# When the second and third piece of one split operand are prepared: with the first or with the second Strassen product of a down projection

## The chip, the cores and the metric

The kernel runs on one core of one Trainium2 chip, as a single launch. The metric is the device time of that launch in microseconds (us); lower is better. Times of whole runs and one profiled execution are used. All instants below are microseconds from the start of the profiled span.

## The reference

One layer of a hybrid encoder on 512 positions of width 1024: a normalised input projection, three token mixers with gates, an output projection with a residual, and then a SwiGLU feed-forward block. The change lies in the last product, `act @ w_ffn_down`, with `D_FF` = 2816:

```python
h2 = rms_norm(x, norm_ffn[l])
act = jax.nn.silu(jnp.einsum('bsd,df->bsf', h2, w_ffn_gate[l])) * jnp.einsum('bsd,df->bsf', h2, w_ffn_up[l])
x = x + jnp.einsum('bsf,fd->bsd', act, w_ffn_down[l])
```

Everything is float32.

## The kernel before

**Products in two parts.** A float32 operand is split into a high part `h`, rounded to the matmul's format by ScalarE (ACT), and a low part `l` = operand − `h`, taken by VectorE (DVE). A product is then three matmuls: high by high, high by low, low by high. Weights are split by `split_a` (lines 1379 and 1380), which writes the pairs named `whd…` and `wld…`; activations of the down projection are split by `split_d2` (lines 1400 and 1401), which writes the tiles named `Bd…`.

**Seven products instead of eight.** The first 256 rows of `w_ffn_down` are multiplied plainly (`fd`, results in `ps_d`). The other 2560 rows are done with a Strassen–Winograd scheme on two by two blocks: products in the order `DORDER` = 11, 12, S1, S2, S3, S4, 22. A product uses five sets of weights (n = 0 to 4) and one split activation operand in three pieces (kh = 0, 1, 2, which hold 4, 4 and 2 slices of 128 rows). Each product is done for two halves of the output, q = 0 and q = 1. In each half three uses of sets stand (`USE`): q = 0 takes sets 0, 1 and the first half of 2, q = 1 the second half of 2, then 3 and 4. A whole set is 24 matmuls of 128x256, a half set 12. `ps_dy` and `ps_dx` are their sums in PSUM.

**Where the activation operands come from.** The operands of the S products are sums and differences of blocks of the activations. They are made in place (`in_place`, line 1570, five DVE instructions for each combination) and then split (`both`, three calls of `split_d2`, one for each kh). The dictionary `LATER` lists, for each product, the pieces of such work that are called while that product is emitted: after each of the three uses, two pieces for q = 0 and one for q = 1. So 9 pieces at most are called with one product; they are taken from the front of its list.

**Where the weights come from.** For products 12 and 22 the sets are loaded by plain DMAs on SyncE's queue (SP) into tiles `dr` of the pool that has three buffers under the tag `raw` (`dfetch`, line 1549). `make_d(n0 + use[0] + 3)` runs ahead of each use: it splits the sets up to three after the one in use and asks for the loads of two more. A `dr` buffer is reloaded when both halves of the split that reads it are done. The weights of the other products stand in tiles `dw`; they are turned into the next combination by DMAs that add in memory, issued by GpSimd (POOL, `dadd`, line 1537). The split weights themselves have three buffers for the high and three for the low parts.

**What sets the order.** A scheduler orders each engine's instructions from the emitted order, their dependencies and priorities. `split_d2` holds the DVE half of a split (line 1401) at its place in the emitted order for all products but 11 and 12 (`tc.keep_in_program_order`, the name `pin`); the ACT half (line 1400) is left free. `in_place` is held too. The DVE halves of the weight splits are held relative to nothing.

`x<-x,ps_dy` (line 1624) is DVE's addition of a finished block to the residual.

Of the kernel before, what the change touches and what calls it, by code (L numbers as in the profile page):

```python
# [12 lines left out]
ALU = mybir.AluOpType  # L13
# [53 lines left out]
def layer_kernel(ctx: ExitStack, tc: tile.TileContext, x, xt, vecs, w_in, w_qkv7, w_gate7, w_pool, w_rg, w_ig,  # L67
# [1184 lines left out]
    with ExitStack() as ffn:  # L1252
# [134 lines left out]
        def ablk(i, kh, j):  # L1387
            return [acts[1 + 5 * i + 2 * kh + n][:, :, j * H:(j + 1) * H] for n in range(2 - kh // 2)]

        def split_d2(nm, kh, i, j):  # L1390

            pin = tc.keep_in_program_order if nm not in ("11", "12") else lambda i: None
            if kh < 2:
                h, l = g4([4, H], f"Bd{nm}{kh}h", F32R), g4([4, H], f"Bd{nm}{kh}l", F32R)
            else:
                t = g4([2, 2, H], f"Bd{nm}{kh}", F32R)
                h, l = t[:, 0], t[:, 1]
            for n, src in enumerate(ablk(i, kh, j)):
                ns = slice(2 * n, 2 * n + 2)
                act(h[:, ns, :], src, AF.Copy)  # L1400
                pin(dve.tensor_tensor(l[:, ns, :], src, h[:, ns, :].bitcast(F32), ALU.subtract))
            DB[nm, kh] = h, l
# [165 lines left out]
        def in_place(dst, sign, op, other):  # L1568
            return [lambda kh=kh: [tc.keep_in_program_order(
                dve.scalar_tensor_tensor(t, t, sign, o, ALU.mult, op)) for t, o in zip(ablk(dst[0], kh, dst[1]), ablk(other[0], kh, other[1]))]  # L1570
                    for kh in range(3)]

        def both(nm, i, j):
            return [lambda kh=kh: split_d2(nm, kh, i, j) for kh in range(3)]
# [4 lines left out]
                   lambda: [dload("21", n, DX) for n in range(5)],  # L1579
                   lambda: [dadd("22", n, DX) for n in range(5)]] + both("12", 1, 0)[:1])  # L1580

        LATER = {"11": both("12", 1, 0)[1:] + in_place((0, 0), 1.0, ALU.subtract, (0, 1)) + both("S1", 0, 0),
                 "12": in_place((0, 0), -1.0, ALU.subtract, (1, 1)) + both("S2", 0, 0),
                 "S1": in_place((0, 1), -1.0, ALU.add, (1, 1)) + both("S3", 0, 1),
                 "S2": both("S4", 1, 1) + in_place((0, 0), -1.0, ALU.subtract, (1, 0)),
                 "S3": both("22", 0, 0)}
# [50 lines left out]
        for nm in DORDER:  # L1637
            z, half, first, adds = plan[nm]
            todo = LATER.get(nm, [])
            n0 = dsets.index((nm, 0))  # L1640
# [76 lines left out]
```

## Time and profile before

| | us |
|---|---|
| median of 3 runs | 901.95 |
| lowest and highest of them | 900.20 and 902.67 |
| the profiled execution's own time | 900.52 |
| its span, first to last instruction | 898.7 |
| PE (TensorE matmul) busy | 891.1 |
| DVE busy | 736.7 |
| ACT busy | 532.9 |
| POOL busy | 106.7 |

In a timeline a row is: start, duration, engine, line, operation, output <- inputs, shapes, count; in brackets stands how long the engine was idle before it and what released it. Rows of equal neighbours are merged ("x4"). Engines start the next instruction a little before the profile's end of the last one, so a row's distance to the next start is what it occupies. PE's busy share counts matmuls whose ends are modelled, so a matmul's row is longer than its distance to the next.

### The profile page before, as it was taken

Reading aid. Unit: us, or ns where it says so; the run is one execution under the profiler, and the core shown is the slowest. Engines: PE = TensorE matmul, PEld = TensorE weight load, DVE = VectorE, ACT = ScalarE, POOL = GpSimd, SP = SyncE. Lnnn points to the kernel's source line nnn. Section 1 sums busy time; section 2 is a strip of 40 time slices with the busy share of each in tenths; the row PEclk is TensorE's granted clock in tenths of the full one; section 3 lists DMA queues with packets and bytes.
Section 4 is the critical chain, followed back from the end, with each engine's and each line's share of the span. In section 5 each row is a group of like instructions: output and inputs, shape, how many; then the busy total and the mean of one; then the engine's idle time right before and its main releaser. Section 6 shows DMA issues by size and latency. Waiting matters only on the chain.

```text
span 898.7 us, 14578 instructions
## 1 busy us (share of the span) xinstructions
PE 891.1 (99%) x5731; PEld 802.4 (89%) x5731; DVE 736.7 (82%) x937; ACT 532.9 (59%) x747; POOL 106.7 (12%) x150
## 2 busy tenths in 40 slices
PE   9999999999999999999999999999999999998998
PEld 6888778888899888888888988999999999998998
DVE  7897897988786599967887685798888888998974
ACT  7554989556856556555664545655555555654642
POOL 1010002232332101000001100000010100121200
PEclk9999999999999999999999999999999999999999
DMA  9485347798582786634635864836666676887913
GB/s 342 141 309 150 114 132 210 220 299 244 179 262 71 234 234 192 218 118 145 214 93 154 190 179 164 258 81 174 169 148 176 162 169 201 211 210 205 196 39 117
DMA packets 83620, 164.59 MB, mean 183 GB/s; under 512 B 7904, under 2 KB 48864, under 8 KB 83552
## 3 DMA queue, kind: packets, MB, share of 16 engines
q1 hardware_dynamic: 68000, 107.29, 35.9%
q0 software_dynamic: 15408, 56.11, 28.2%
q8 instruction: 45, 0.74, 0.3%
q10 hardware_dynamic: 144, 0.26, 0.1%
q14 instruction: 23, 0.19, 0.1%
HBM read 143.19 MB, written 18.87 MB: 180 GB/s over the span
## 4 chain that ended last, share of the span: by engine, by line
PE 93%; DVE 3%; ACT 2%; DMA 1%; issue 1%; DVEq 0%; ACTq 0%; SPq 0%
PE ps_y L283 13%; PE ps_x L283 10%; PE ps_q L794 7%; PE ps_dy L1633 5%; PE ps_dx L1633 4%; PE ps_br L274 3%; PE ps_br L275 3%; PE ps_br L276 3%; PE ps_bY L1234 2%; PE ps_gy L283 2%; PE ps_gate L697 2%; PE ps_gate L276 2%; PE ps_bX L1234 2%; PE ps_gx L283 2%; PE ps_gate L274 2%; PE ps_gate L275 2%
## 5 line engine op out<-in xcount | busy, mean ns | idle before, releaser
L110 ACT ACTIVATE whi<-raw 128x1024 fp32r<-128x1024 f32 x61 | 64.6, 1059 | 73.3 <-PE ps_br L275 14.7
L111 DVE TENSOR_TENSOR wlo<-raw,whi 128x1024 fp32r<-128x1024 f32 x61 | 74.4, 1220 | 28.9 <-ACT whi L110 28.9
L111 DVE TENSOR_TENSOR wlo<-qw,whi 128x1024 fp32r<-128x1024 f32 x48 | 58.6, 1222 | 20.8 <-ACT whi L110 20.4
L110 ACT ACTIVATE whi<-qw 128x1024 fp32r<-128x1024 f32 x48 | 50.7, 1057 | 33.1 <-PE ps_q L794 18.7
L1379 ACT ACTIVATE wh<-w 128x1024 fp32r<-128x1024 f32 x34 | 36.2, 1064 | 49.4 <-PE ps_x L283 24.7
L1380 DVE TENSOR_TENSOR wl<-w,wh 128x1024 fp32r<-128x1024 f32 x34 | 41.6, 1223 | 7.3 <-ACT wh L1379 6.7
L1380 DVE TENSOR_TENSOR wl_S<-w,wh_S 128x1024 fp32r<-128x1024 f32 x30 | 36.6, 1220 | 12.1 <-ACT wh_S L1379 12.0
L1379 ACT ACTIVATE wh_S<-w 128x1024 fp32r<-128x1024 f32 x30 | 31.8, 1060 | 22.5 <-PE ps_y L283 19.8
L1379 ACT ACTIVATE whdS<-dw 128x1024 fp32r<-128x1024 f32 x20 | 21.3, 1064 | 22.1 <-PE ps_dy L1633 11.1
L1380 DVE TENSOR_TENSOR wldS<-dw,whdS 128x1024 fp32r<-128x1024 f32 x20 | 24.2, 1220 | 6.4 <-ACT whdS L1379 6.3
L1050 DVE TENSOR_TENSOR_SCAN E<-K,ahead 128x512 f32<-128x512 f32 (+3 forms) x32 | 25.3, 812 | 4.4 <-ACT K L1046 4.4
L274 PE MATMUL ps_br<-yHH,whi 128*128 128x512 f32 x64 | 25.3, 395 | 0.0
L274 PE MATMUL ps_lru<-HH,whi 128*128 128x512 f32 x64 | 25.2, 394 | 0.0
L274 PE MATMUL ps_br<-yph,whi 128*128 128x512 f32 x64 | 25.2, 394 | 0.0
L274 PE MATMUL ps_pool<-HH,whi 128*128 128x512 f32 x64 | 25.2, 393 | 0.0
L274 PE MATMUL ps_gate<-HH,whi 128*128 128x512 f32 x64 | 25.0, 391 | 0.0
L276 PE MATMUL ps_gate<-HH,wlo 128*128 128x512 f32 x64 | 25.0, 391 | 0.0
L275 PE MATMUL ps_br<-ypl,whi 128*128 128x512 f32 x64 | 25.0, 391 | 0.0
L276 PE MATMUL ps_br<-yph,wlo 128*128 128x512 f32 x64 | 25.0, 391 | 0.0
L275 PE MATMUL ps_br<-yHL,whi 128*128 128x512 f32 x64 | 25.0, 390 | 0.0
L276 PE MATMUL ps_br<-yHH,wlo 128*128 128x512 f32 x64 | 25.0, 390 | 0.0
L275 PE MATMUL ps_pool<-HL,whi 128*128 128x512 f32 x64 | 25.0, 390 | 0.0
(768 smaller groups left out, 3540.0 us busy)
## 6 DMA issues: line engine op xcount, KB each, us to landing
w<-in_w_gu_dram SPq DMA_DIRECT2D x44, 512.0 KB, 6.6
raw<-in_w_in_dram SPq DMA_DIRECT2D x31, 512.0 KB, 5.2
qw<-in_w_qkv_dram SPq DMA_DIRECT2D x24, 512.0 KB, 6.5
w<-in_w_gu_dram POOLq DMA_DIRECT2D x20, 512.0 KB, 7.3
dw<-in_w_down_dram POOLq DMA_DIRECT2D x20, 512.0 KB, 8.0
raw<-in_w_branch_dram SPq DMA_DIRECT2D x16, 512.0 KB, 4.2
qw<-in_w_qkv_dram POOLq DMA_DIRECT2D x12, 512.0 KB, 7.8
qd<-r POOLq DMA_DIRECT2D x12, 512.0 KB, 7.8
```

What stands on the lines that cost most here:

```text
L110: act(hi, raw, AF.Copy)
L111: dve.tensor_tensor(lo, raw, hi.bitcast(F32), ALU.subtract)
L274: nc.tensor.matmul(ps, lh, rh, start=start, stop=False, skip_group_check=skip)
L275: nc.tensor.matmul(ps, lh, rl, start=False, stop=False, skip_group_check=skip)
L276: nc.tensor.matmul(ps, ll, rh, start=False, stop=stop, skip_group_check=skip)
L283: nc.tensor.matmul(o, a_[a][:, w, k, :], b_[b][:, k, :], start=first and n == k == 0, stop=last and n == 2 and k == 3, skip_group_check=True)
L794: nc.tensor.matmul(ps[:, a, :], b_[:, k, ts_], a_[:, kk, :], start=first and n == k == 0, stop=n == 2 and k == 3, skip_group_check=True)
L1050: dve.tensor_tensor_scan(E[:, c0:c0 + n][:, ::-1], K[:, c0 + 1:c0 + n + 1][:, ::-1], ahead[:, S - n:][:, ::-1], 0.0, ALU.mult, ALU.add)
L1234: nc.tensor.matmul(o, ah[x_][:, w, k, :], b[k][y_], start=first_ and n == k == 0, stop=n == 2 and k == 3, skip_group_check=True)
L1379: act(h, src, AF.Copy)
L1380: dve.tensor_tensor(l, src, h.bitcast(F32), ALU.subtract)
L1633: nc.tensor.matmul(o, a_[a][:, w, k0 + k, :], b_[b][:, k, :], start=first and i == k == 0, stop=last and i == 2 and k == nk - 1, skip_grou ...
```

## The change

In `LATER`, two of the three calls that split the operand of S1 (kh = 1 and kh = 2) move from the end of the list of product 11 to the front of the list of product 12. The first (kh = 0) stays with 11. No instruction is added or removed.

```diff
-        LATER = {"11": both("12", 1, 0)[1:] + in_place((0, 0), 1.0, ALU.subtract, (0, 1)) + both("S1", 0, 0),
-                 "12": in_place((0, 0), -1.0, ALU.subtract, (1, 1)) + both("S2", 0, 0),
+        LATER = {"11": both("12", 1, 0)[1:] + in_place((0, 0), 1.0, ALU.subtract, (0, 1)) + both("S1", 0, 0)[:1],
+                 "12": both("S1", 0, 0)[1:] + in_place((0, 0), -1.0, ALU.subtract, (1, 1)) + both("S2", 0, 0),
```

The list of 11 goes from 8 pieces to 6, that of 12 from 6 to 8. As built, the queues differ only in this stretch:

- DVE, before: BdS11l (two instructions), wld120, BdS12, wld121, the addition `x<-x,ps_dy` of q = 1, wld122, four of the five in-place differences for S2, wld123, the fifth, BdS20l (two), wld124, BdS21l (two), BdS22, wldS10, wldS11.
- DVE, after: wld120, wld121, the addition, wld122, BdS11l (two), BdS12, wld123, four in-place differences, wld124, the fifth, BdS20l (two), BdS21l (two), wldS10, BdS22, wldS11.
- ACT, before: BdS10h (two), whd120, BdS11h (two), whd121, BdS12, whd122, whd123, BdS20h (two), whd124, BdS21h (two), whdS10, BdS22, whdS11.
- ACT, after: BdS10h (two), whd120, BdS11h, whd121, BdS11h, whd122, BdS12, whd123, whd124, BdS20h (two), whdS10, BdS21h (two), BdS22, whdS11.
- PE: before, two matmuls of q = 1 with set 122 stood ahead of the third matmul of product 12's first set; after, they stand with the others of set 122.
- POOL and SP: the same instructions in the same order.

(Names are product and set or piece: `wld123` is the low part of set 3 of product 12, `BdS11` piece kh = 1 of the operand of S1.)

## The prediction

> **What bounds the kernel now.** I read the page first, for the span and the chain of work that ended last; then that chain in order of time, to see where it leaves PE; then the timelines of PE, DVE and ACT there; and last the stretches with PE's clock and the DMA queues.
>
> ```profile
> span 898.7 us, 14578 instructions
> ...
> PE 93%; DVE 3%; ACT 2%; DMA 1%; issue 1%; DVEq 0%; ACTq 0%; SPq 0%
> ```
>
> The profiled execution took 900.52 us, 1.8 more than this span, and the chain is PE for 93% of it. An edit to DVE's order is worth something only where the chain leaves PE. From 780 us on that is one place, between the first two products of the down projection. PE's own rows there:
>
> ```profile
> 808.83 0.28 PE L1633 MATMUL ps_dx<-Bd120l,whd 128*128 128x256 f32 x1
> 809.96 0.51 PE L1633 MATMUL ps_dx<-Bd,whd 128*128 128x256 f32 x2 [0.85 <-ACT whd L1379]
> ...
> 817.90 0.28 PE L1633 MATMUL ps_dx<-Bd,wld 128*128 128x256 f32 x1
> 818.98 0.39 PE L1633 MATMUL ps_dx<-Bd120h,whd 128*128 128x256 f32 x1 [0.81 <-ACT whd L1379]
> 819.21 0.28 PE L1633 MATMUL ps_dx<-Bd120l,whd 128*128 128x256 f32 x1
> 820.24 0.39 PE L1633 MATMUL ps_dx<-Bd120h,wld 128*128 128x256 f32 x1 [0.76 <-DVE wld L1380]
> ...
> 827.41 0.28 PE L1633 MATMUL ps_dx<-BdS10h,wldS 128*128 128x256 f32 x1
> ```
>
> The same stretch by PE's clock:
>
> ```profile
> 817.52:820.93 3.41, 1.84 (x13) 1.44 (x13) 1.97 (x3) 2.77 (x4) 0.00 (x0) 1.00 0.61 243
> 820.93:824.37 3.44, 3.44 (x19) 3.44 (x18) 3.44 (x6) 2.89 (x5) 0.00 (x0) 0.51 0.60 166
> 824.37:828.00 3.63, 3.63 (x34) 3.63 (x34) 2.84 (x3) 1.80 (x2) 1.34 (x2) 0.99 0.33 132
> ```
>
> (Columns: stretch, length, PE, PEld, DVE, ACT, POOL busy with counts, granted clock, DMA share, GB/s.)
>
> At full clock matmuls of this size start 0.11 us apart (34 in 3.63). So PE stands three times: about 1.0 us before 809.96, 0.97 before 818.98 and 0.9 before 820.24. The last row is the third matmul of S1, the first that needs wldS10; I use it as the finish line, because from there PE runs without a stop.
>
> What PE waits for at 818.98 and 820.24 is set 123, and that set's load starts the wait:
>
> ```profile
> 810.04 7.72 DMA dr<-in_w_down_dram
> ```
>
> It is issued at 810.04 and lands at 817.76. It could not be issued earlier: its buffer is that of set 120, and was free only when DVE had made wld120. DVE's rows (I read them for what stands ahead of what):
>
> ```profile
> 806.96 0.68 DVE L1624 TENSOR_TENSOR x<-x,ps_dy 128x512 f32<-128x512 f32 x1
> 807.56 1.28 DVE L1401 TENSOR_TENSOR BdS11l<-act,BdS11h 128x512 fp32r<-128x512 f32 x2
> 808.76 1.22 DVE L1380 TENSOR_TENSOR wld<-dr,whd 128x1024 fp32r<-128x1024 f32 x1
> 809.90 0.68 DVE L1401 TENSOR_TENSOR BdS<-act,BdS 128x512 fp32r<-128x512 f32 x1
> 810.50 1.21 DVE L1380 TENSOR_TENSOR wld<-dr,whd 128x1024 fp32r<-128x1024 f32 x1
> 811.64 0.68 DVE L1624 TENSOR_TENSOR x<-x,ps_dy 128x512 f32<-128x512 f32 x1
> 812.24 1.22 DVE L1380 TENSOR_TENSOR wld<-dr,whd 128x1024 fp32r<-128x1024 f32 x1
> 813.37 2.49 DVE L1570 SCALAR_TENSOR_TENSOR act<-act,act 128x512 f32<-128x512 f32 x4
> 818.96 1.23 DVE L1380 TENSOR_TENSOR wld<-dr,whd 128x1024 fp32r<-128x1024 f32 x1 [3.10 <-ACT whd L1379]
> 820.10 0.68 DVE L1570 SCALAR_TENSOR_TENSOR act<-act,act 128x512 f32<-128x512 f32 x1
> 820.71 1.28 DVE L1401 TENSOR_TENSOR BdS20l<-act,BdS20h 128x512 fp32r<-128x512 f32 x2
> 821.91 1.22 DVE L1380 TENSOR_TENSOR wld<-dr,whd 128x1024 fp32r<-128x1024 f32 x1
> 823.05 1.28 DVE L1401 TENSOR_TENSOR BdS21l<-act,BdS21h 128x512 fp32r<-128x512 f32 x2
> 824.25 0.68 DVE L1401 TENSOR_TENSOR BdS<-act,BdS 128x512 fp32r<-128x512 f32 x1
> 824.85 2.35 DVE L1380 TENSOR_TENSOR wldS<-dw,whdS 128x1024 fp32r<-128x1024 f32 x2
> ```
>
> DVE is full here but for 3.10 us ahead of 818.96, and the four in-place differences at 813.37 are done before that gap. By the distances of starts, a weight split occupies 1.14, a half split or a difference 0.60, two of them 1.20, four 2.40.
>
> **The change, part by part.** *Wld120 moves ahead of BdS11l.* It starts at 807.56 instead of 808.76 and ends at 808.78. The load of set 123 follows 0.06 behind as now: issued at 808.84, 1.20 earlier. wld121 then stands at 808.70, and wld122 behind the addition at about 810.44. PE needs wld121 24 matmuls (2.7 us) after 808.9 and wld122 as long again after that, so both are early.
>
> *PE's stop at 809.96 goes.* It was for whd122, out of turn: two matmuls of set 122 stood ahead of the third of set 120. In the changed queue they stand in their place, and wld120 is there at 808.78. PE goes on at 808.95 and comes to set 123 1.01 earlier, at 817.00 instead of 818.01. That alone buys nothing: it lengthens the wait for set 123.
>
> *Set 123 comes earlier.* If the load takes 7.72 again, it lands at 816.56. From landing to PE's matmul with wld123 the chain is ACT, then DVE, 2.48 now (817.76 to 820.24) and 2.48 then: 819.04. Here PE is 1.20 ahead.
>
> *The differences for S2 now stand behind wld123.* This is the new wait. BdS11l and BdS12 take the place ahead of the gap (wld122 starts at 810.44, so they end by about 813.4), and DVE then waits for whd123 until 817.76 with four differences queued behind it. They are not waiting for the load, but the queue is in order. DVE's gap grows from 3.10 to over 4 us, and 2.40 of work moves behind it. Behind wld123 (at 817.76) come, in the changed order: four differences at 818.90, wld124 at 821.30, the fifth at 822.44, BdS20l at 823.04, BdS21l at 824.24, wldS10 at 825.44, done at 826.66. BdS22 (0.60) goes behind wldS10, which is already counted. PE meets this twice: at wld124 (wanted at 821.8, there at 822.52), then at wldS10 (wanted at 825.3, there at 826.66). S1's third matmul starts 0.04 later, at **826.70 instead of 827.41: 0.71 less**.
>
> ACT's halves do not bind: its rows show it waiting for data.
>
> ```profile
> 817.87 1.06 ACT L1379 ACTIVATE whd<-dr 128x1024 fp32r<-128x1024 f32 x1 [7.97 <-DMA dr<-in_w_down_dram]
> 818.84 1.14 ACT L1400 ACTIVATE BdS20h<-act 128x512 fp32r<-128x512 f32 x2
> 820.26 1.06 ACT L1379 ACTIVATE whd<-dr 128x1024 fp32r<-128x1024 f32 x1 [0.29 <-DMA dr<-in_w_down_dram]
> ```
>
> Even if set 124 landed no earlier than the 820.2 it now has, whd124 would end at 821.32, and wld124 stands at 821.30 anyway. The moved pieces themselves cost nothing later: BdS11 and BdS12 are wanted at S1's second and third set, after 829, and are made by 813.4. POOL's and SP's instructions keep their order. PE's, ACT's and DVE's work is the same, so the sum is this 0.71 and nothing else.
>
> *The clock.* The three stretches above change what 0.71 is compared with. After the two stops the clock is halved for 3.44 us, and 19 matmuls start where 34 do next. [...] Without the halving, PE in the kernel before would have used wld124 at 823.17 and wldS10 when it was done (824.85 + 1.22 = 826.07): finish line 826.11, that is 1.30 earlier. In the changed kernel a halving between 819 and 826 hides in the 2 us that PE waits for DVE anyway. So against an execution before without it, the change costs 826.70 − 826.11 = 0.59; against the profiled one it gains 0.71. A halving later, inside S1, is hidden by nothing.
>
> The unknown is the load. Around its issue the queues hold:
>
> ```profile
> 800.67 3.57 POOL L1537 DMA_DIRECT2D dw<-in_w_down_dram  x4 [12.86 <-DMA dw<-in_w_down_dram]
> ```
> ```profile
> q0 software_dynamic: 68, 0.21, 108.9%
> ```
> ```profile
> q0 software_dynamic: 57, 0.17, 86.3%
> q1 hardware_dynamic: 14, 0.06, 15.1%
> ```
> ```profile
> DMA to landing us min/median/max: 3.3/5.7/8.7
> ```
>
> The second fence is the stretch 810 to 811, the third 813 to 814: POOL's additions (q0) hold the DMA engines alone for 3 us after the issue, and only then do the load's packets (q1) begin. The last is all `dr` loads. So the load could land where it does now, 817.76, if it has to wait for the same additions; or earlier by more than 1.20, if an earlier place in the queue is worth one 512 KB addition, 0.524 MB at the 0.21 MB per us of the second fence, 2.5 us. I take its own 7.72 again.
>
> **The rivals.** *The load does not move (slower).* It waits for the additions and lands at 817.76. For it: the 3 us without a packet. Against: loads elsewhere do not wait so, down to 3.3 us. DVE's wld123 stays at 818.96 and everything behind it comes 1.20 later than in my sum: wldS10 done at 827.86, finish 827.90, 0.49 more than the profiled run, 1.79 more than one without the halving. It decides from a landing at 817.27, where my 0.71 is used up.
>
> *The halving falls into S1 (slower).* The two stops ahead of 826.70 are about 0.7 and 1.4 us, in 5 us; if one stretch of 3.4 holds as much of them as 817.52:820.93 did, S1 runs 3.44 us at half: 16 matmuls instead of 30, 1.6 us. Then +0.9 against the profiled run. Against it: the stops are further apart than now.
>
> *The load gains a whole addition (faster).* It lands 2.5 earlier, at 815.26; DVE's chain then moves 1.30 further, unless set 124 holds it: finish 825.4, 2.0 less. [...]
>
> *It does nothing.* ACT's halves hardly move, and if PE's gain ends in a stall of equal size, the time is that of before.
>
> **How the numbers follow.** Forecast 0.52; load unmoved 0.18; halving in S1 0.15; whole addition 0.10; nothing 0.05. On the profiled time: 900.52 − 0.71 = 899.81. The median of the three runs is 1.43 above that execution; the same 0.71 less than 901.95 gives **901.2**. The rivals by the same median: 902.4, 902.9, 899.9 and 902.0. Three runs of the kernel before spread over 2.47 us (0.27%), so 0.3%, 2.7 us, is about what can be told from no change. No case alone reaches it: the largest are −2.0 and, against runs of before without the halving, +1.8 (load unmoved) and +2.2 (halving in S1). Beyond it lie only these joined with the runs' own spread, or an unmoved load and a halving in S1 together (+2.1 on the profiled run). I give faster by over 0.3% 0.10, within 0.76, slower 0.14, and the range **899.0 to 904.4**: from 899.9 down by 0.9 and from 902.9 up by 1.5, for the spread.
>
> **What would show it.** In the changed profile: PE without a stop near 809; the load of set 123 issued near 808.8 and its landing; DVE idle over 4 us ahead of wld123 with four L1570 behind it; PE waiting for DVE at wld124 and wldS10, the latter done about 7.7 us after wld123; and where the clock is halved. I am wrong if the finish line moves by more than 2 us, if PE stops in S1 or later for DVE, or if the work ahead of 800 us differs.

## The result, and the profile after

| | before | after |
|---|---|---|
| median of 22 runs each (us) | 900.22 | 902.80 |
| lowest and highest (us) | 898.89, 904.26 | 901.75, 905.75 |
| profiled execution, its span (us) | 900.52, 898.7 | 902.23, 900.5 |

The ratio of after to before is 1.0022, with a 95% interval of 1.0012 to 1.0032. The change makes the kernel slower, by about 0.2%. The forecast was 0.7 us faster. The time lies in the range and within the 0.3% that the prediction called the limit of what can be told, but the sign is the other one. Two later comparisons of the same instruction order gave 1.0008 [0.9995, 1.0021] and 1.0001 [0.9988, 1.0014], so the loss by medians lies between nothing and 0.3%.

The page of after:

```profile
span 900.5 us, 14576 instructions
```

PE's timeline between the first two products of the down projection (start, duration, engine, line, operation, output <- inputs; in brackets the idle time before and its releaser):

```profile
817.42 0.28 PE L1633 MATMUL ps_dx<-Bd,wld 128*128 128x256 f32 x1
820.03 0.38 PE L1633 MATMUL ps_dx<-Bd120h,whd 128*128 128x256 f32 x1 [2.34 <-ACT whd L1379]
820.25 0.28 PE L1633 MATMUL ps_dx<-Bd120l,whd 128*128 128x256 f32 x1
821.29 0.58 PE L1633 MATMUL ps_dx<-Bd120h,wld 128*128 128x256 f32 x1 [0.76 <-DVE wld L1380]
...
828.32 0.28 PE L1633 MATMUL ps_dx<-BdS10l,whdS 128*128 128x256 f32 x1
828.98 0.38 PE L1633 MATMUL ps_dx<-BdS10h,wldS 128*128 128x256 f32 x1 [0.38 <-DVE wldS L1380]
```

No stop is left near 809: PE reaches set 123 early, and then stands 2.34 us for it instead of 0.81. The last row is the finish line of the prediction. It stands at 828.98; before it was 827.41. PE has a new wait there, for wldS10. About 0.33 of the 1.57 us is older than the change: the first matmul of the down projection starts at 794.96 in this execution and at 794.62 in the one before.

The chain of waits that ended last, in order of time (start, duration, what):

```profile
808.25 1.14 DVE wld L1380
...
809.41 9.41 DMA dr<-in_w_down_dram
...
818.92 1.06 ACT whd L1379
...
820.01 1.24 DVE wld L1380
...
821.29 6.50 PE ps_dx L1633 x42
827.79 1.15 DVE wldS L1380
...
828.98 13.66 PE ps_dx L1633 x118
```

The load of set 123 is issued 0.63 earlier than before (809.41 against 810.04). It takes 9.41 us instead of 7.72 and lands at 818.82, 1.05 later. After it DVE is in the chain twice: for wld123, and 6.5 us later for wldS10. DVE's timeline between the two:

```profile
813.37 0.69 DVE L1401 TENSOR_TENSOR BdS<-act,BdS 128x512 fp32r<-128x512 f32 x1
820.01 1.23 DVE L1380 TENSOR_TENSOR wld<-dr,whd 128x1024 fp32r<-128x1024 f32 x1 [5.95 <-ACT whd L1379]
821.15 2.49 DVE L1570 SCALAR_TENSOR_TENSOR act<-act,act 128x512 f32<-128x512 f32 x4
823.56 1.22 DVE L1380 TENSOR_TENSOR wld<-dr,whd 128x1024 fp32r<-128x1024 f32 x1
824.70 0.69 DVE L1570 SCALAR_TENSOR_TENSOR act<-act,act 128x512 f32<-128x512 f32 x1
825.30 1.29 DVE L1401 TENSOR_TENSOR BdS20l<-act,BdS20h 128x512 fp32r<-128x512 f32 x2
826.50 1.29 DVE L1401 TENSOR_TENSOR BdS21l<-act,BdS21h 128x512 fp32r<-128x512 f32 x2
827.71 1.22 DVE L1380 TENSOR_TENSOR wldS<-dw,whdS 128x1024 fp32r<-128x1024 f32 x1
```

DVE is idle for 5.95 us, with four differences that wait for nothing but their turn behind wld123. From wld123 to wldS10 it is full.

What holds the load, by the DMA queues (queue, packets, MB, share of 16 engines). The first answer is the stretch from 809.5 to 813, the second that from 813 to 819:

```profile
q0 software_dynamic: 196, 0.74, 106.1%
...
dr<-in_w_down_dram SPq DMA_DIRECT2D x3, 512.0 KB, 9.4
```
```profile
q0 software_dynamic: 182, 0.61, 52.4%
q1 hardware_dynamic: 313, 1.16, 50.5%
```

Three loads have been issued by the end of the first stretch, and not one packet of theirs (q1) moves in it. The DMA engines work off additions (q0) that POOL had issued long before:

```profile
801.29 3.57 POOL L1537 DMA_DIRECT2D dw<-in_w_down_dram  x4 [12.27 <-DMA dw<-in_w_down_dram]
806.14 0.85 POOL L1537 DMA_DIRECT2D dw<-in_w_down_dram  x1 [1.28 <-DVE wld L1380]
```

These five are the last set of one combination (22) and sets 1 to 4 of the next (product 11's buffers, for S3). By the completion events in the trace they land at 806.51, 809.19, 811.64, 814.64 and 819.13, and the load at 818.82. Before, they landed at 806.20, 808.80, 811.31, 813.79 and 817.59, and the load at 817.77.

Last, the clock (stretch, length, PE, PEld, DVE, ACT, POOL busy with counts, granted clock, DMA share, GB/s):

```profile
817.58:820.99 3.41, 0.61 (x3) 0.30 (x2) 0.98 (x1) 1.69 (x2) 0.00 (x0) 1.00 0.73 288
820.99:824.41 3.42, 3.12 (x14) 3.12 (x15) 3.42 (x6) 2.96 (x5) 0.00 (x0) 0.50 0.45 153
```

It is halved at the same place as before, and for as long: 3.41 us, from 820.99 here and from 821.02 there.

### The profile page after: what moved, and what is told of

Read it like the earlier page. It is cut to its first block, busy times and chain, and to the rows that moved or that the text cites. A ratio compares the mean times of both kernels' runs of the same rounds, so it can differ in the third digit from the quotient of the medians.

```text
span 900.5 us, 14576 instructions
## 1 busy us (share of the span) xinstructions
PE 891.7 (99%) x5731; PEld 802.5 (89%) x5731; DVE 736.6 (82%) x937; ACT 532.9 (59%) x747; POOL 106.6 (12%) x150
## 4 chain that ended last, share of the span: by engine, by line
PE 93%; DVE 3%; ACT 2%; DMA 1%; issue 1%; DVEq 0%; ACTq 0%
PE ps_y L283 13%; PE ps_x L283 10%; PE ps_q L794 7%; PE ps_dy L1633 5%; PE ps_dx L1633 4%; PE ps_br L274 3%; PE ps_br L276 3%; PE ps_br L275 3%; PE ps_gate L697 2%; PE ps_bY L1234 2%; PE ps_gy L283 2%; PE ps_gate L276 2%; PE ps_bX L1234 2%; PE ps_gx L283 2%; PE ps_gate L274 2%; PE ps_gate L275 2%
```

## The experiments

My theory after the result: the load of set 123 lands with the last of the additions, whatever its time of issue, and the differences behind wld123 then cost DVE 2.4 us. The rivals: the load is slow by itself; the differences alone do it; the loss is in the clock.

### The two halves of the change, each alone

The change does two things: weights 120 to 122 go ahead of BdS11l on DVE, and four differences go behind wld123. One kernel keeps the first and puts the differences back ahead of wld123 (edit of the changed kernel):

```diff
-                 "12": both("S1", 0, 0)[1:] + in_place((0, 0), -1.0, ALU.subtract, (1, 1)) + both("S2", 0, 0),
+                 "12": [lambda: [f() for f in both("S1", 0, 0)[1:] + in_place((0, 0), -1.0, ALU.subtract, (1, 1))[:1]]]
+                 + in_place((0, 0), -1.0, ALU.subtract, (1, 1))[1:] + both("S2", 0, 0),
```

> The changed kernel with one more edit: the S1 pieces and the first in-place difference are called as one, so that DVE has early weights (wld120 to wld122 ahead of BdS11l, as in the change) and four differences ahead of wld123 (as before the change). Theory A (the differences queued behind wld123 cost the time, the early load gives nothing): the time of the kernel before, ratio 0.999 to 1.001; the load of set 123 still lands with POOL's fifth addition, near 817.6 to 819. Rival B (the early load itself does harm, because it shares the DMA engines with the additions for longer): slower by about 1 us or more, ratio 1.001 to 1.002, as the changed kernel. Rival C (a halved clock inside S1): the ratio of the changed kernel only in those runs that show a second halving.

One keeps the order of before and only puts the differences behind wld123 (`nothing` is an empty call; edit of the kernel before):

```diff
-                 "12": in_place((0, 0), -1.0, ALU.subtract, (1, 1)) + both("S2", 0, 0),
+                 "12": 2 * [nothing] + in_place((0, 0), -1.0, ALU.subtract, (1, 1)) + both("S2", 0, 0),
```

> The kernel before with two empty pieces at the front of the list of product 12: the weights stay late (wld120 behind BdS11l) but four differences move behind wld123, as in the changed kernel. Theory A: as slow as the changed kernel or nearly so: 0.7 us over a run of before that has the halved clock, 1.8 over one that has not; ratio 1.001 to 1.002. Rival B: the time of before, ratio 0.9995 to 1.0005. On the profile, A expects DVE idle for about 5 us ahead of wld123, four L1570 behind it and PE waiting for wldS10.

One moves the third piece (kh = 2) alone (shown against the changed kernel):

```diff
-... + both("S1", 0, 0)[:1],
+... + both("S1", 0, 0)[:2],
-                 "12": both("S1", 0, 0)[1:] + ...
+                 "12": both("S1", 0, 0)[2:] + ...
```

> Only the last third (kh = 2) of S1's split moves to product 12. As built: wld120 stays behind BdS11l; wld121 and wld122 come one half split earlier; two differences stand ahead of wld123 and three behind it, where before had four and one, and the changed kernel none and five. Theory A: between the two, 0.1 us over a run of before with the halved clock and 1.2 over one without, ratio 1.000 to 1.0015. Rival B: as before, ratio 0.9995 to 1.0005, because the load of set 123 is issued when it was.

And the changed kernel once more beside them:

> The changed kernel once more, beside the others on the same chip. It was 1.0022 [1.0012, 1.0032] of before. Theory A and rival B both expect 1.001 to 1.003. For the profile, theory A expects the load of set 123 to land within 0.5 us of POOL's fifth addition (817.8 and 817.6 before, 818.8 and 819.1 after), whenever it was issued; a load that keeps its 7.7 us would land near 816.6.

| | median (us) | lowest, highest | ratio to before [95%] |
|---|---|---|---|
| early weights, differences ahead | 901.19 | 900.23, 904.71 | 0.9991 [0.9976, 1.0005] |
| late weights, differences behind | 902.39 | 901.42, 905.76 | 1.0009 [0.9995, 1.0023] |
| one third moved | 901.58 | 900.98, 906.17 | 0.9997 [0.9981, 1.0013] |
| the change again | 902.44 | 901.46, 903.26 | 1.0008 [0.9995, 1.0021] |
| before, beside them | 902.45 | 899.05, 904.88 | |

No interval excludes 1. The profiles say more than the times. With the differences ahead of wld123 (the chain in order of time; one line is added in this kernel, so L1633 is L1634):

```profile
810.05 9.05 DMA dr<-in_w_down_dram
...
820.30 1.24 DVE wld L1380
...
821.58 3.00 PE ps_dx L1634 x24
...
824.62 16.61 PE ps_dx L1634 x142
```

Its load lands 0.28 later than that of after, and still DVE leaves the chain after wld123 but for 0.3 us at 824.6; the wait for wldS10 is gone. So that wait comes from the place of the differences, as the prediction said. Repeats of both orders (below) agree: PE is idle 0.35 and 0.33 us before that matmul in the changed order, and not at all in this one. With one third moved a wait for wldS10 is there as well, and longer, 1.05 us against 0.38 in after; ahead of it the granted clock was 1.00 from 817.5 to 828 in that execution (PE's timeline):

```profile
828.38 0.39 PE L1633 MATMUL ps_dx<-BdS10h,wldS 128*128 128x256 f32 x1 [1.05 <-DVE wldS L1380]
```

In all four the load took 7.70 to 9.33 us. The profile of the second (late weights, differences behind) had a further stop of 2.0 us near 798 for a load of product 11; it was the slowest of its twelve runs. DVE is idle for 7.12 us ahead of wld123 there, with four differences behind it, as expected. But the wait for wldS10 that was expected with them is missing: PE ran 6.83 us at half clock from 823.56 on and reached that matmul only at 832.65, after DVE had made wldS10 at 831.85.

### The load without the additions

The kernel before, with the additions behind product 11 left out:

```diff
-                if nm in NEXT:
+                if nm in NEXT and nm != "11":
```

> The kernel before without POOL's five additions that follow the sets of product 11 (so S3 gets weights that are not combined; this part of the computation is left out). If these additions hold the load of set 123, it lands 3.5 to 5 us after its issue instead of 7.7, PE no longer stops for set 123, and no clock is halved there: 2.5 to 4 us less than before, ratio 0.996 to 0.9975, with PE's stop of 1 us at 809 still there. If the load's time comes from something else, it stays near 7.7 us and the ratio near 1.

Measured: 897.51 us (897.08 to 901.28), ratio 0.9957 [0.9938, 0.9976]. ACT's timeline shows set 123 there 3.63 us after ACT had done the one ahead of it:

```profile
814.38 1.07 ACT L1379 ACTIVATE whd<-dr 128x1024 fp32r<-128x1024 f32 x1 [3.63 <-DMA dr<-in_w_down_dram]
```

The load is issued at 810.80 and lands at 814.28, in 3.48 us. PE's stops near 818 and 820 are gone, and with them the halved stretch; the stop near 809 stays. The load is not slow by itself.

### Additions emitted later, and put back by the scheduler

To keep the additions and move them, three kernels (order of before, changed order, changed order with the differences ahead of wld123) emitted them with sets 3 and 4 of product 12:

```diff
-                if nm in NEXT:
+                if nm in NEXT and nm != "11":
...
+                if (nm, n) in (("12", 3), ("12", 4)):
+                    for i in ((0, 1) if n == 3 else (2, 3, 4)):
+                        dadd("21", i, DY)
```

> The kernel before, with the same five additions called with the last two sets of product 12 instead of with the sets of 11; nothing is left out. Theory: set 123 lands early, PE keeps only the stop at 809, ratio 0.996 to 0.998, unless the additions then delay those of S1, whose results S2 wants near 838: each takes 2.5 us, so up to 5 us of a new stop ahead of S2 or S3 would show as PE waiting for whdS.

> The changed kernel with the additions moved in the same way. Without the load's stop, the change's own terms are left: PE's stop at 809 gone (1.0 less), four differences behind wld123 (PE waits 0.4 to 0.6 for wldS10). Theory A: 0.3 to 0.6 us less than the kernel before with late additions, so the same change is then a small gain. Rival B (early weights do harm through the additions): no harm left either, same numbers; a loss of 1 us or more against it would speak against both.

> Early weights, four differences ahead of wld123 (as in the first experiment) and late additions: none of the three stops is left, so about 1.1 us less than the kernel before with late additions; ratio 0.995 to 0.997 of before, the fastest of all.

The edit did not reach the queues: nothing keeps an addition from being issued as soon as its buffer is free, and the scheduler put them where they had been. POOL's timeline of the second of them has the same two rows as that of after:

```profile
801.37 3.57 POOL L1537 DMA_DIRECT2D dw<-in_w_down_dram  x4 [12.28 <-DMA dw<-in_w_down_dram]
806.25 0.85 POOL L1537 DMA_DIRECT2D dw<-in_w_down_dram  x1 [1.31 <-DVE wld L1380]
```

So these are repeats of before, after and the first experiment: 901.98 (0.9999 [0.9984, 1.0015]), 901.92 (1.0001 [0.9988, 1.0014]) and 902.84 us (1.0007 [0.9991, 1.0023]), with before at 901.58 beside them. None of what the expectations built on a moved addition was tried by them. They show how far single profiles of one order lie apart: from the first matmul of the down projection to the last one's start the order of before took 100.45 us and, here, 103.52 (with 6.83 us at half clock); the changed order took 101.81, 101.58 and 101.03.

### Additions held behind set 123

Here the five additions for S3 wait, by an explicit dependency (`SYNC`, a semaphore; `dadd` now returns its instruction), until ACT has made whd123. The same edit in the order of before, in the changed order, and in the changed order with the differences ahead; and the changed order with the additions left out.

```diff
-            act(h, src, AF.Copy)
+            highs.append(act(h, src, AF.Copy))
...
-                if nm in NEXT:
-                    m, buf = NEXT[nm]
-                    dadd(m, n, buf)
+                for i in range(5) if (nm, n) == ("12", 3) else [n] if nm in ("S1", "S2") else []:
+                    m, buf = NEXT[nm] if nm != "12" else NEXT["11"]
+                    (a := dadd(m, i, buf)) and nm == "12" and tc.add_manual_dep(a.ins, highs[-1].ins.name, SYNC, reason="set 123")
```

> The order of the kernel before; the five in-memory additions that make the weights of the next product (sets 0 to 4 of product 11's buffers) wait on POOL until whd123 has been made, that is until the load of set 123 is done with. Nothing is left out. Theory (the load lands with the last queued addition, whenever it is issued): with only the addition of 22's last set in the queue the load takes about 3.5 us as in the run without additions, set 123 lands near 814.5, the two stops of PE near 818 and 820 are gone, the stop near 809 (about 1.1) stays; first down matmul to last PE end 97 us instead of 100.4; 898 to 899 us, 0.4% below the kernel before. If the additions only move and hold the next load or S1's sets instead, the stops come back at S1 and the time is that of before, 901 to 902. If the load itself is slow (no matter what is queued), set 123 still takes 7 to 9 us.

> The changed order with the same delay of the additions as the run beside it; nothing is left out. Theory: the forecast's step, an earlier issue is an earlier landing, is right only where no additions stand in the way. Then set 123 is issued near 809.2 and lands near 813, wld123 is made before PE asks for it, the four differences behind it cost nothing, and the stop near 809 is gone as well: about 1 us less than the same delay in the order of before, first down matmul to last PE end near 96 us, 897 to 898 us. Rival: the differences behind wld123 cost their 2.4 us of DVE in any case: then 1 to 2 us above the run beside it, with PE waiting for wldS10.

> The changed order of weights, the four differences ahead of wld123, with the same delay of the additions; nothing is left out. Theory: with set 123 there in time the place of the differences is no matter: within 0.3 us of the changed order with the same delay (897 to 898 us). Rival (the place of the differences matters by itself): more than 1 us below it.

> The changed order without the five additions behind product 11 (that part is left out). Theory: the load of set 123 takes 3 to 4 us from its issue near 809.3, there is no stop near 809, 818 or 820, and the stage from the first down matmul to the last PE end is about 1.0 us shorter than the 96.7 of the order of before without the additions: the change is then a gain, about 0.1%. Rival: the differences behind wld123 make PE wait for wldS10 all the same: then 1 us or more longer than 96.7.

| | median (us) | ratio to before [95%] |
|---|---|---|
| held, order of before | 904.40 | 1.0023 [1.0008, 1.0037] |
| held, changed order | 901.70 | 1.0005 [0.9990, 1.0021] |
| held, changed, differences ahead | 900.82 | 0.9995 [0.9979, 1.0011] |
| no additions, changed order | 896.79 | 0.9945 [0.9925, 0.9965] |

The load took 3.36 to 3.54 us in all four, and no stop near 818 or 820 was left. But the three times expected of the held additions were missed by 3 to 6 us. The first chain shows where it went:

```profile
809.94 9.30 PE ps_dx L1633 x80
...
823.31 13.21 DMA dw<-in_w_down_dram
...
836.62 1.06 ACT whdS L1379
...
838.85 1.23 DVE wldS L1380
```

The addition that makes S2's first set is issued at 823.31 behind the held ones, takes 13.21 us, and PE's starts are 0.8 and 2.2 us apart at S2's first set, near 838. What was won near 818 was given back 20 us later. The other two have 2.1 and 1.9 us there. With the differences ahead the median is 0.88 below that of the changed order; the intervals overlap, so the third expectation is neither borne out nor refuted. The changed order is 2.70 us below that of before, where about 1 was expected; those two intervals overlap as well, and each has a stop at S2, so this does not price the change. Without the additions neither stop exists, and the expectation for the pair was right: from the first matmul of the down projection to the last one's start it is 95.85 us in the changed order and 96.71 in that of before, 0.86 less.

### Additions behind those of S1

What was held is needed only by S3, whose matmuls start after 850. So it can stand behind the additions of S1, which make S2's weights and are more urgent (`ORDER` fixes the order in POOL's queue and waits for nothing):

```diff
-                if nm in NEXT:
-                    m, buf = NEXT[nm]
-                    dadd(m, n, buf)
+                last = dadd(NEXT[nm][0], n, NEXT[nm][1]) if nm in ("S1", "S2") else None
+                for i in range(5) if (nm, n) == ("S1", 4) else []:
+                    tc.add_manual_dep(dadd("21", i, DY).ins, last.ins.name, ORDER, reason="behind S1's additions")
```

> The order of the kernel before; the five additions that make S3's weights (buffers of product 11) are queued on POOL behind the five of S1 that make S2's. Nothing is left out. Theory: the load of set 123 takes 3.4 us and there is no stop near 818 or 820, and S2's additions are not held, so no stop near 838 either; only the stop near 809 (1.1) is left. First down matmul to last PE end 96.7 as without the additions, 897.5 to 898.5 us, ratio 0.996. If S3's weights now come late: a stop near 849 of 1 to 3 us and 899 to 901.

> The changed order with the additions behind S1's as in the run beside it; nothing is left out. Theory (the forecast's step is right where the load is free): also no stop near 809, first down matmul to last PE end 95.9, 0.9 less than the order of before, 896.5 to 897.5 us, ratio 0.995. Rival (the differences behind wld123 cost 2.4 of DVE in any case): PE waits for wldS10 near 826 and the stage is 97 to 98.5.

Measured: in the order of before 898.00 us (896.97 to 898.43, 8 runs), ratio 0.9952 [0.9934, 0.9971]; in the changed order 897.85 us (895.92 to 902.24, 12 runs), ratio 0.9958 [0.9938, 0.9979]. Both are about 4 us faster than before (901.98 beside them) and leave nothing out. The page and the chain of the second:

```profile
span 894.7 us, 14575 instructions
```
```profile
798.26 11.25 PE ps_dy L1633 x94
809.52 27.33 PE ps_dx L1633 x240
836.85 27.20 PE ps_dy L1633 x240
864.05 13.60 PE ps_dx L1633 x120
877.65 10.20 PE ps_dy L1633 x90
887.85 3.41 PE ps_dx L1633 x30
```

From 798.26 to the end of the down projection the chain is PE alone. In the order of before one stop is left in it, the 1.1 us near 809:

```profile
811.10 0.50 PE L1633 MATMUL ps_dx<-Bd,whd 128*128 128x256 f32 x2 [0.85 <-ACT whd L1379]
```

The four differences stand behind wld123 in the changed order here too, and cost nothing, because wld123 is made at once (DVE's timeline):

```profile
813.48 0.68 DVE L1401 TENSOR_TENSOR BdS<-act,BdS 128x512 fp32r<-128x512 f32 x1
814.23 1.22 DVE L1380 TENSOR_TENSOR wld<-dr,whd 128x1024 fp32r<-128x1024 f32 x1
815.38 2.49 DVE L1570 SCALAR_TENSOR_TENSOR act<-act,act 128x512 f32<-128x512 f32 x4
```

First matmul of the down projection to the last one's start: 97.04 us in the order of before, 96.00 in the changed order, 1.04 less (0.9 expected). The lowest runs differ by 1.05 as well, the medians by only 0.15, and 897.85 lies above the 896.5 to 897.5 expected: four of the twelve runs of the changed order took 899.6 to 902.2, with a granted clock of 0.999 or 1.000. What they waited for isn't in the one profile; it stays open. So that the changed order is faster here is shown for the profiled executions and the lowest runs, not for the medians.

## Why the prediction was wrong

**The step that failed** is "If the load takes 7.72 again". The load of set 123 in all sixteen profiles:

| additions for S3 | order | issued | landed | took | last queued addition landed |
|---|---|---|---|---|---|
| as before | before | 810.04 | 817.77 | 7.73 | 817.59 |
| as before | before (emitted later) | 811.24 | 820.25 | 9.01 | 818.83 |
| as before | after | 809.41 | 818.82 | 9.41 | 819.13 |
| as before | after, again | 809.61 | 818.84 | 9.23 | 819.50 |
| as before | after (emitted later) | 809.52 | 818.50 | 8.98 | 819.65 |
| as before | early weights, differences ahead | 810.05 | 819.10 | 9.05 | 820.23 |
| as before | the same (emitted later) | 809.27 | 818.80 | 9.53 | 819.12 |
| as before | late weights, differences behind | 812.41 | 821.74 | 9.33 | 821.57 |
| as before | one third moved | 811.12 | 818.82 | 7.70 | 818.61 |
| out, held or behind S1's | seven profiles, issued 809.52 to 811.26 | | | 3.36 to 3.54 | 803.65 to 805.28 |

With the additions in the queue the load takes 7.7 to 9.5 us and lands between 1.2 us before and 1.4 us after the last of them; without them it takes 3.4 to 3.5. The packets in the trace show two parts. In all nine profiles with the additions the load's first packet moves 3.61 to 3.75 us after the issue (3.66 in before, 3.68 in after), for issues from 809.27 to 812.41; in the seven without it is 0.96 to 0.98. So an earlier issue does start the load earlier: at 813.09 in after, at 813.70 in before. But its bytes then took 5.73 us instead of 4.07, beside additions that ended no sooner.

Counted from the first matmul of the down projection, the load is issued at 14.1 to 14.5 us in the five profiles with early weights, and at 15.4 to 16.1 in three with wld120 late (the fourth has the stop near 798). It lands at 23.1 to 23.9 and at 23.1 to 25.0. On average 1.5 us at the issue became 0.4 at the landing, less than profiles of one order differ.

The same load took between 3.36 and 9.53 us here, so its 7.72 could not be carried over to another time of issue. This was the prediction's own rival, "the load does not move", which had 0.18. Its evidence was quoted there: the stretch of 3 us after the issue with no packet of the load. I set against it that other loads of `dr` come in 3.3 us, which have no additions ahead of them; the price should have come from rows with the same queue.

**The other terms, by the prediction's own list.**

- *PE's stop at 809 goes*: right. PE runs from 809 to 817.42 without a stop. The load was issued 0.57 later than forecast (809.41 against 808.84), 0.33 of which is the later start of the stage.
- *The differences stand behind wld123*: right in size. From wld123's start to wldS10's are 7.70 us in the trace; the forecast's rows give 7.68 (817.76 to 825.44).
- *PE meets this twice, at wld124 and at wldS10*: half right. wld124 was done at 824.78, PE asked for it at 825.62, after a halved stretch. Only wldS10 stopped PE.
- *The finish line*: 826.70 forecast, 828.98 measured. The rival gave 827.90 for a landing at 817.76; the landing was 1.05 later than before, about 0.33 of it by the later start of the stage, and 827.90 + 1.05 = 828.95.
- *The load gains a whole addition*: fell. The four profiles with an issue before 810.04 landed at 818.50 to 818.84, none before the 817.77 of before. Once the load's packets had begun, both queues moved: 1.16 MB of loads and 0.61 MB of additions from 813 to 819 in after. No run shows the gain of a whole addition, 2.5 us, and the equal wait of 3.61 to 3.75 us ahead of the first packet stays unexplained.
- *The halving falls into S1*: fell in the profiled execution of after, where it begins at 820.99 and ends at 824.41.

**A second step, the base.** The profiled execution of before had a halved stretch, and the forecast was made against it. The prediction gave the other base too: against one without the halving the change costs 0.59, and with the load unmoved 1.79. Four later comparisons give the mean granted clock of each run of before, and three give that of the changed order. In the profiles of before and after one halved stretch goes with 0.998; in the three profiles with 6.83 us at half clock it is 0.996.

| granted clock | before: runs, median (us) | after: runs, median (us) |
|---|---|---|
| 0.999 or 1.000 | 70, 900.83 | 6, 902.56 |
| 0.998 | 33, 902.84 | 27, 902.28 |
| 0.997 or less | 15, 903.77 | 13, 903.26 |

Of before, 70 of 118 runs have 0.999 or more; of after, 6 of 46. In the first row, where after has only 6 runs, the change costs 1.73 us; in the second it gains 0.56. The median of all 46 runs of after, 902.58, is 1.75 above the runs of before without a halving, for the rival's 1.79. That the two lie so close is in part luck: the 70 runs spread from 898.98 to 906.28. After, the runs at 0.998 are no slower than those above (902.28 against 902.56), as the prediction said: PE waits for DVE in that place anyway, 0.38 us for wldS10 in the profile with the halved stretch. So the sign depends in part on how many runs of before are halved. That this is what sets 1.0022, 1.0008 and 1.0001 apart is not shown: for the first, the clocks of the runs of before are not on record, and in the other two 17 of 35 and 24 of 34 runs of before had 0.999 or more, which would order them the other way. The table pools runs of several chips, so it shows the pattern, not a tenth of a microsecond.

The profiled run of before ran 3.41 us at half clock behind stops of 0.97 and 0.9 us, and 48 of 118 runs of it have a granted clock of 0.998 or less. What decides whether a run is halved is not shown.

**What was right**: the wait that moves, its place in DVE's queue and its price, and that PE's stop at 809 goes. With the load free the order is a gain, 0.86 and 1.04 us in two pairs of profiles. That is near the 0.71 of the forecast, but by another path: there nothing is left to gain from an earlier landing, and what goes is the stop at 809, which the prediction said buys nothing alone.

## What to carry to other kernels

The latency of the load went here with what stood in the DMA engines ahead of it: 3.36 to 3.54 us with no addition left, 7.70 to 9.53 with some. So before an earlier issue is counted as an earlier landing, find whose packets move in the time between, and whether they end sooner too. Work put behind a wait in an engine's queue delayed here what stands behind it by its full time: from wld123 to wldS10 it was 7.70 us in after and 5.89 in before, with 2.40 of differences more between them and 0.60 of BdS22 less. It cost nothing where the wait was gone. When queued transfers are moved out of the way of one load, put them behind the next urgent transfer, not just behind that load (in the order of before 898.00 us against 904.40), and take a base from more than one execution where the granted clock differs between runs of one kernel (0.996 to 1.000 in those of before).

## What the runs showed of the hardware

- A load of 512 KB on SP's queue took 3.36 to 3.54 us with no addition ahead (seven profiles), and 7.70 to 9.53 with some of POOL's additions of 512 KB still to do (nine profiles; 7.73 in before, 9.41 in after). Its first packet moved 0.96 to 0.98 us after the issue without them and 3.61 to 3.75 us with them (3.66 in before, 3.68 in after). The additions themselves landed 2.45 to 2.68 us apart in before and after while they had the engines alone, and the last one 3.8 (before) and 4.5 us (after) behind the one ahead of it while loads moved beside it.
- After stops of like size the granted clock was halved in some executions and not in others. In before, PE's starts lay 1.08 and 1.03 us apart at its two stops near 818 and 820, and 3.41 us at a clock of 0.50 followed from 821.02 on; in after 2.61 and 1.04 us, and 3.41 us at 0.50 from 820.99 on. In the profile with early weights and the differences ahead there were stops of 2.30 and 1.04 us (818.02 to 820.32, 820.54 to 821.58), and the mean granted clock of that execution was 0.999, against 0.998 in before and after. In the one with one third moved PE was busy for 2.29 of 3.40 us from 817.5 on (1.84 of 3.41 in before), and the clock was 1.00 up to 828. In the one with late weights and the differences behind it was 0.50 for 6.82 us from 823.56 on. What sets this off is not shown; no run tested it.
